# DeltaNet heads: the chunk output moved into the bank of values and state, the freed bank to the scores, three kinds of copies from VectorE to ScalarE

## The chip, the cores and the metric

One core of a Trainium2 chip. The metric is device microseconds (us) of one execution; 3 executions of the kernel before were timed. Engines: PE (TensorE, matmuls), DVE (VectorE), ACT (ScalarE), POOL (GpSimd), SP (SyncE, which issues most DMAs). Matmul results lie in PSUM, whose eight banks hold 512 fp32 numbers per partition each.

## What is computed

One step of a two-layer backbone: 128 context and 512 latent tokens, width 1024. Layer 0 runs softmax attention and a bidirectional gated DeltaNet side by side; layer 1 is a Mamba-2 mixer; each layer ends in an MLP. The change lies in the DeltaNet heads (four of them, key and value width 128). Per head and direction, over chunks:

```python
kb = k * beta[..., None]
m = where(strict, einsum('bnhid,bnhjd->bnhij', kb, k) * decay, 0.0)
t_mat = triangular_solve(eye + m, eye, lower=True, unit_diagonal=True)
u = t_mat @ (v * beta[..., None])
w = t_mat @ (kb * exp(gc)[..., None])
def step(s, inp):
    u_c, w_c, qk_c, qd_c, kd_c, dec_c = inp
    v_new = u_c - w_c @ s                  # the corrected values
    o_c = qd_c @ s + qk_c @ v_new          # the chunk's output
    s = s * dec_c[..., None, None] + einsum('bhcd,bhce->bhde', kd_c, v_new)
    return s, o_c
```

The kernel uses chunks of 128 tokens: one for the context, four for the latents. Then o is RMS-normalised and gated, laid beside the attention's output, and both go through one output projection.

## The kernel before

The large products (L287) are made of three passes, high and low parts of both operands, and PE is busy with them for most of the span. The change touches one stage, from about 225 to 525 us: four DeltaNet heads (`delta_head`, L768) are issued between the steps of the attention (`attention`, L1072, a generator) in the order 0, attention, 1, 2, 3 (the string in `even`). Heads 0 and 2 use one set of buffers and PSUM banks, heads 1 and 3 the other. A pool's buffer is given to the next tile when its last reader is done, so head 2 starts step by step as head 0 gives its tiles free.

Attention: per head pair a front (transposes L1114, scores L1124, maxima on DVE L1131 and L1136) and a back (scores again, L1154, exponentials on ACT, values L1182, and small products that close it, L1190 and L1198). Scores, their transposes and L1198 use the pool psc, which has two banks.

A head: matrix M (L806), inverse X by blocks (L821 to L924), w (L933), then eight steps, four chunks in both directions (L940 to L964): a bank `pv` takes v_new (L945, L946, both PE); DVE reads it twice, as vk (L949) and as vn (L951); L953 puts the state's product into the same bank and L955 adds it to the state; a bank of its own, `ops` of the one-bank pool pdno, takes the output (L957, L958), which ACT (L962) or DVE (L964) reads. The context's chunk follows (L969 to L982), then the finish: five squares (ACT L987), the reciprocal root (L988 and small DVE operations), scaling (DVE L996), transposes (PE L997) and the gate (DVE L998).

The output projection L287 needs weights split by ACT (L263) and DVE (L266), and operands split by ACT (L510) and DVE, among them the heads' outputs; head 2's end frees the room of operand 5. The reload of x (L663) is issued on ACT's queue.

The order of the instructions on each engine is set when the program is built, by a scheduler that simulates its own timeline (`schedule_with_timeline_sim`, L1617); the engines then work through their lists in order. Banks are given in the order of the pools. The stage before has pg1 (3 banks), pm1 (2, for the transposes `kvps`, L721), pmod1 (1) and pat0 (1).

Of the kernel before, what the change touches and what calls it, by code (L numbers as in the profile page):

```python
# [11 lines left out]
F32 = mybir.dt.float32  # L12
F32R = mybir.dt.float32r
I32 = mybir.dt.int32
AF = mybir.ActivationFunctionType
ALU = mybir.AluOpType
# [4 lines left out]
P = 128  # L21
# [171 lines left out]
class Prog:  # L193
# [393 lines left out]
    def even(self):  # L587
        nc, io = self.nc, self.io
# [6 lines left out]
        with ExitStack() as e1:  # L595
# [3 lines left out]
            with ExitStack() as e2:  # L599
# [14 lines left out]
                xs, half = self.modulate(0, ("gmix", 0), 0, 1, hp, xp, True, cuts=4, rbs=rbs)  # L614
# [4 lines left out]
                for b, (n, c0) in enumerate(blocks):  # L619
                    hi, lo = watt[0] if b == 0 else self.wpart(self.wload(("att", b), n, wa), 0, n, wa)  # L620
                    for t in range(NT):
                        ps = self.pg.tile([P, 512], F32, name="atps", tag="g")
                        for k in range(KT):
                            for q, (x, w) in enumerate(((xs[0], hi), (xs[0], lo), (xs[1], hi))):
                                nc.tensor.matmul(ps[:, :n], x[k][:, TOFF[t]:TOFF[t] + P], w[:, k, :],  # L625
                                                 start=k == 0 and q == 0, stop=k == KT - 1 and q == 2)
# [14 lines left out]
                    self.delta_in(tp, pm, h, xs, dn[h])  # L641
        self.share = False
        with eak, ExitStack() as e1:
            cp, *sets, self.pout, psc, pat, at = self.pools(
                e1, ("con2", 1, "right"), ("pdn0", 2, None), ("pdn1", 2, None), ("pdno", 1, None), ("psc", 2, None), ("pat", 1, None), ("at", 1, "left"))
            self.con2 = cp.tile([P, io["cst"].shape[1] - self.csmall], F32, name="con2")
            nc.scalar.dma_start(out=self.con2, in_=io["cst"][:, self.csmall:])
            sets = list(zip(self.pools(e1, ("dn1", 1, "right"), ("dn0", 1, "right")), sets))
            att = self.attention(at, psc, pat, qkv, keys, ota)
            for ch in "0abcdefghi123":  # L650
                if ch in "0123":
                    self.delta_head(*sets[1 - int(ch) % 2], int(ch), dn[int(ch)], gt)
                else:
                    for _ in range(AS):
                        next(att, None)
            for _ in att:
                assert False

        hes, xes, e1 = ExitStack(), ExitStack(), ExitStack()
# [12 lines left out]
        xs, half = self.modulate(0, ("gmlp", 0), 3, 4, hp, np_, False)  # L672
# [95 lines left out]
    def delta_head(self, dn, pd, h, st_, gt):  # L768
        nc, v, g = self.nc, self.nc.vector, self.nc.gpsimd
        qT, kk, vv, zs, rq = (st_[n] for n in ("q", "k", "v", "z", "rq"))  # L770
# [8 lines left out]
        X, Xt = (both(n) for n in ("X", "Xt"))  # L779
# [49 lines left out]
        qd = [dn.tile([P, 4, P], F32, name=f"qd{d}", tag=f"qd{d}") for d in range(2)]  # L829
# [8 lines left out]
        qk = [qk0, dt]  # L838
# [9 lines left out]
        def values(d, t):  # L848

            o = dn.tile([P, P], F32, name="vb", tag=f"vb{d}")  # L850
            nc.scalar.activation(out=o, in_=vv[:, t, :], func=AF.Copy, scale=gt["beta"][:, d, t, h:h + 1])
            return o
# [27 lines left out]
        for l in range(1, 5):  # L880
            py = bank()
            for t in range(NT):
# [3 lines left out]
                            in1=lev[:, l - 1:l, 0].rearrange("p o (b c) -> p o b c", c=32).to_broadcast(wide), op=ALU.mult)  # L886
# [3 lines left out]
            for e in range(2):  # L890
                v.scalar_tensor_tensor(out=Xtc[:, e], in0=pu[:, :NT * 64].rearrange("p (t e c) -> p t e c", e=2, c=32)[:, :, e, :],
                                       scalar=lvn[:, l - 1, e:e + 1], in1=Xtc[:, e], op0=ALU.mult, op1=ALU.add)
# [19 lines left out]
        half = lambda ps: ps[:, :NT * H].rearrange("p (t c) -> p t c", c=H)  # L912
        for d in range(2):
            a, b = hv[d], hv[1 - d]
# [4 lines left out]
        for d in range(2):  # L919
            a, b = hv[d], hv[1 - d]  # L920
            pz = bank()
            for t in range(NT):
                nc.tensor.matmul(pz[a, t * H:(t + 1) * H], W[a, t, a], Yc[a, t, b], start=True, stop=True)
            v.tensor_scalar(out=X[a, 1 - d, :, b], in0=half(pz)[a], scalar1=-1.0, scalar2=None, op0=ALU.mult)  # L924

        o = M
        wn = (Xt[:, 0], kT)
# [7 lines left out]
        st = []  # L935
# [4 lines left out]
        for n in range(4):  # L940
            for d in range(2):
                c = n if d == 0 else 3 - n
                t = c + 1
                pv = bank()
                nc.tensor.matmul(pv[:, 0:P], X[:, 1 - d, t, :], values(d, t), start=True, stop=False)  # L945
                nc.tensor.matmul(pv[:, 0:P], wn[d][:, t, :], st[d], start=False, stop=True)  # L946
                if n < 3:
                    vk = dn.tile([P, P], F32, name="vk", tag=f"vk{d}")
                    v.tensor_scalar(out=vk, in0=pv[:, 0:P], scalar1=gt["ek"][:, d, t, h:h + 1], scalar2=None, op0=ALU.mult)  # L949
                vn = dn.tile([P, P], F32, name="vn", tag=f"vn{d}", bufs=2)  # L950
                v.tensor_copy(vn, pv[:, 0:P])  # L951
                if n < 3:
                    nc.tensor.matmul(pv[:, P:2 * P], kk[:, t, :], vk, start=True, stop=True)  # L953
                    s = dn.tile([P, P], F32, name="s", tag=f"s{d}", bufs=2)
                    v.scalar_tensor_tensor(out=s, in0=st[d], scalar=dec[d][:, c:c + 1], in1=pv[:, P:2 * P], op0=ALU.mult, op1=ALU.add)  # L955
                po = self.pout.tile([P, 512], F32, name="ops", tag="o")
                nc.tensor.matmul(po[:, 0:P], qd[d][:, c, :], st[d], start=True, stop=False)  # L957
                nc.tensor.matmul(po[:, 0:P], qk[d][:, t, :], vn, start=False, stop=True)  # L958
                if n < 3:
                    st[d] = s  # L960
                if n < 2:
                    nc.scalar.activation(out=o[:, t, :], in_=po[:, 0:P], func=AF.Copy, scale=rq[:, t:t + 1])  # L962
                else:
                    v.scalar_tensor_tensor(out=o[:, t, :], in0=po[:, 0:P], scalar=rq[:, t:t + 1], in1=o[:, t, :], op0=ALU.mult, op1=ALU.add)  # L964

        vns = []
        for d in range(2):
            pv = bank()
            nc.tensor.matmul(pv[:, 0:P], X[:, 1 - d, 0, :], values(d, 0), start=True, stop=True)  # L969
            vk = dn.tile([P, P], F32, name="vk", tag=f"vk{d}")  # L970
            v.tensor_scalar(out=vk, in0=pv[:, 0:P], scalar1=gt["ek"][:, d, 0, h:h + 1], scalar2=None, op0=ALU.mult)
            vn = dn.tile([P, P], F32, name="vn0", tag=f"vn{d}", bufs=2)
            v.tensor_copy(vn, pv[:, 0:P])
            vns.append(vn)
            nc.tensor.matmul(pv[:, P:2 * P], kk[:, 0, :], vk, start=True, stop=True)
            s = dn.tile([P, P], F32, name="s0", tag=f"s{d}", bufs=2)
            nc.scalar.copy(out=s, in_=pv[:, P:2 * P])
            nc.sync.dma_start(out=self.io["o_sd"][d, h], in_=s)
        po = bank()
# [646 lines left out]
```

## Time and profile before

| | us |
|---|---|
| median of 3 executions | 2215.07 (2214.77 to 2222.48) |
| profiled execution, its own time | 2212.08 |
| its span | 2210.0 |
| PE busy | 2101.8 |
| DVE busy | 1340.5 |
| ACT busy | 911.9 |
| mean granted TensorE clock | 0.978 of full |

In the rows further down, "busy" is the time in which an engine had an instruction in work; PEld is the loading of weights, which goes on beside PE. PEclk is the clock granted to TensorE as a share of 2.4 GHz. "Idle before" is an engine's idle time just ahead of a group's instructions, with the operation that ended it. "x10" counts records; an fp32 matmul of this stage has two. Names such as dps (the heads' banks), scps (scores), kvps and ops are those of the tiles.

### The profile page before, as it was taken

What the parts mean: (1) busy time and instruction counts of PE and PEld (TensorE: products, weight loads), DVE (VectorE), ACT (ScalarE), POOL (GpSimd) and SP (SyncE); (2) the same over time, 40 slices, a digit from 0 to 9 for tenths busy, and PEclk for the clock granted to TensorE, in tenths of its full rate; (3) what the DMA queues carried; (4) which work ended last, traced back from release to release, by engine and by line L of the source; (5) the groups of instructions that cost most, each with busy time, mean ns of one, the idle gap of its engine ahead of it and who ended that gap; (6) DMA issues with size and microseconds to landing.
All of it is one profiled execution on the core that took longest, in us unless ns stands there. A gap on an engine that the chain in (4) does not pass through costs nothing.

```text
span 2210.0 us, 36682 instructions
## 1 busy us (share of the span) xinstructions
PE 2101.8 (95%) x15045; PEld 1982.5 (90%) x15045; DVE 1340.5 (61%) x2751; ACT 911.9 (41%) x1914; POOL 224.1 (10%) x138
## 2 busy tenths in 40 slices
PE   6999798999999999999989899999899999999997
PEld 5999686888899999999888788989899899999996
DVE  6486767655786777663767665676653733334344
ACT  4345445352532323242466566666521522222230
POOL 1041403100000000000111112222310000000000
PEclk9999898899999999999999999999999999999999
DMA  7351101003254444421245343444322221122211
GB/s 319 119 194 39 38 1 34 1 19 149 88 190 142 153 138 149 150 98 44 93 126 136 102 123 104 110 134 120 100 102 77 77 77 72 67 73 76 77 58 48
DMA packets 70792, 221.93 MB, mean 100 GB/s; under 512 B 6266, under 2 KB 39010, under 8 KB 49762
## 3 DMA queue, kind: packets, MB, share of 16 engines
q1 hardware_dynamic: 60464, 205.10, 28.0%
q10 hardware_dynamic: 10162, 14.50, 1.9%
q8 instruction: 118, 1.93, 0.4%
q14 instruction: 48, 0.39, 0.1%
HBM read 211.40 MB, written 8.18 MB: 99 GB/s over the span
## 4 chain that ended last, share of the span: by engine, by line
PE 79%; DVE 8%; DMA 7%; ACT 3%; issue 1%; SPq 1%; ACTq 0%; DVEq 0%; POOL 0%; POOLq 0%
PE gps L287 61%; DMA bc<-afs 3%; DMA Q<-afs 3%; PE atps L625 2%; PE avps L1182 2%; PE stps L448 1%; PE yps L1523 1%; DMA wraw<-wall 1%; ACT bc L1508 1%; PE scps L1124 1%; PE dps L883 1%; DMA X<-growd 1%; PE stps L1552 1%; PE dps L889 1%; PE modps L331 1%
## 5 line engine op out<-in xcount | busy, mean ns | idle before, releaser
L287 PE MATMUL gps<-hh,whi 128*128 128x322 f32 (+3 forms) x1552 | 493.3, 318 | 1.2 <-ACT whi L263 0.9
L287 PE MATMUL gps<-hh,wlo 128*128 128x322 f32 (+3 forms) x1552 | 489.4, 316 | 1.3 <-POOL wlo L266 0.8
L287 PE MATMUL gps<-hl,whi 128*128 128x322 f32 (+3 forms) x1552 | 487.4, 314 | 2.2 <-DVE hl L505 2.2
L263 ACT CAST whi<-wraw 128x1024 fp32r<-128x1024 f32 (+2 forms) x220 | 231.7, 1056 | 516.3 <-PE gps L287 493.3
L287 PE MATMUL gps<-hidh,whi 128*128 128x320 f32 x1024 | 317.4, 310 | 0.0
L287 PE MATMUL gps<-hidl,whi 128*128 128x320 f32 x1024 | 316.1, 309 | 0.0
L287 PE MATMUL gps<-hidh,wlo 128*128 128x320 f32 x1024 | 315.8, 308 | 0.0
L287 PE MATMUL gps<-yh,whi 128*128 128x320 f32 x1280 | 304.3, 309 | 1.8 <-ACT yh L1264 1.8
L287 PEld LDWEIGHTS gps<-hh,whi 128*128 128x128 f32 (+1 forms) x1552 | 294.1, 190 | 9.6 <-issue 6.0
L287 PEld LDWEIGHTS gps<-hl,whi 128*128 128x128 f32 (+1 forms) x1552 | 294.0, 189 | 6.4 <-DVE hl L505 3.2
L287 PEld LDWEIGHTS gps<-hh,wlo 128*128 128x128 f32 (+1 forms) x1552 | 294.3, 190 | 4.7 <-issue 2.5
L266 DVE TENSOR_TENSOR wlo<-wraw,whi 128x1024 fp32r<-128x1024 f32 (+1 forms) x185 | 230.8, 1249 | 73.2 <-ACT whi L263 72.8
L287 PE MATMUL gps<-yh,wlo 128*128 128x320 f32 x768 | 237.6, 310 | 0.0
L517 DVE SCALAR_TENSOR_TENSOR xt<-gps,mod,xt 128x128 f32<-128x128 f32 (+1 forms) x216 | 87.9, 436 | 227.4 <-PE gps L287 227.3
L287 PEld LDWEIGHTS gps<-yh,whi 128*128 128x128 f32 x1280 | 220.0, 188 | 3.6 <-ACT yh L1264 1.9
L287 PEld LDWEIGHTS gps<-hidh,whi 128*128 128x128 f32 x1024 | 192.1, 188 | 2.8 <-issue 1.6
L287 PEld LDWEIGHTS gps<-hidl,whi 128*128 128x128 f32 x1024 | 192.1, 188 | 1.0 <-issue 1.0
L287 PEld LDWEIGHTS gps<-hidh,wlo 128*128 128x128 f32 x1024 | 192.1, 188 | 0.0
L266 POOL TENSOR_TENSOR wlo<-wraw,whi 128x1024 fp32r<-128x1024 f32 (+1 forms) x35 | 93.2, 2663 | 950.1 <-ACT whi L263 933.4
L287 PEld LDWEIGHTS gps<-yh,wlo 128*128 128x128 f32 x768 | 144.9, 189 | 0.1
L352 DVE SCALAR_TENSOR_TENSOR macc<-wraw,condst,macc 128x512 f32<-128x512 f32 x196 | 136.9, 744 | 1.2 <-ACT macc L355 1.2
L530 DVE TENSOR_SCALAR hr<-gps 128x320 f32<-128x320 f32 x128 | 62.6, 489 | 109.4 <-PE gps L287 109.3
(398 smaller groups left out, 3338.7 us busy)
## 6 DMA issues: line engine op xcount, KB each, us to landing
wraw<-wall SPq DMA_DIRECT2D x158, 1024.0 KB, 4.9
bc<-afs SPq DMA_DIRECT2D x40, 512.0 KB, 6.5
Q<-afs SPq DMA_DIRECT2D x64, 128.0 KB, 7.2
xt<-xt ACTq DMA_DIRECT2D x2, 2560.0 KB, 11.6
X<-growd SPq DMA_DIRECT2D x8, 320.0 KB, 6.1
xd<-xt ACTq DMA_DIRECT2D x1, 2560.0 KB, 8.5
xt<-xd SPq DMA_DIRECT2D x1, 2560.0 KB, 10.3
S<-ss ACTq DMA_DIRECT2D x16, 128.0 KB, 2.2
```

The costliest lines, as they stand in the source:

```text
L263: self.nc.scalar.copy(out=hi, in_=raw[:, :, c:c + m])
L266: eng.tensor_tensor(out=lo, in0=raw[:, :, c:c + m], in1=hi.bitcast(F32), op=ALU.subtract)
L287: self.nc.tensor.matmul(ps, ws[k // KT][q // 2][:, k % KT, :], xs[q % 2][k][:, c], start=k == 0 and q == 0, stop=k == n - 1 and q == 2)
L331: nc.tensor.matmul(ps[32 * q:32 * q + 32], lhs, x[:, :, 32 * q:32 * q + 32], start=start, stop=stop)
L352: nc.vector.scalar_tensor_tensor(out=a, in0=x, scalar=w, in1=a, op0=ALU.mult, op1=ALU.add)
L448: pin = nc.tensor.matmul(ps[r:r + 32, :HU], self.ones32, sq, start=k < 4, stop=k >= nk - 4)
L517: self.nc.vector.scalar_tensor_tensor(out=x[:, dst], in0=ps[:, src], scalar=gate[:, m, q:q + 1], in1=x[:, dst], op0=ALU.mult, op1=ALU.add)
L530: nc.vector.tensor_scalar(out=r, in0=ps, scalar1=0.0, scalar2=None, op0=ALU.max)
L625: nc.tensor.matmul(ps[:, :n], x[k][:, TOFF[t]:TOFF[t] + P], w[:, k, :], start=k == 0 and q == 0, stop=k == KT - 1 and q == 2)
L883: nc.tensor.matmul(py[:, t * 32:(t + 1) * 32], m32[:, t, :], mixed(Xc, t, l), start=True, stop=True)
L889: nc.tensor.matmul(pu[:, t * 64:(t + 1) * 64], Yc[:, t, :], Xtc[:, :, t, :], start=True, stop=True)
L1182: nc.tensor.matmul(acc, val(c, i), p, start=c == 1, stop=c == 6)
```

## The change

The pool pdno goes; a chunk's output is written into columns 256 to 383 of the bank that holds v_new and the state's product. The freed bank is psc's third. The copy vn of the corrected values (L951, and L973 for the context) and the negated half of the inverse (L924) are made by ACT in place of DVE.

```diff
-            cp, *sets, self.pout, psc, pat, at = self.pools(
-                e1, ("con2", 1, "right"), ("pdn0", 2, None), ("pdn1", 2, None), ("pdno", 1, None), ("psc", 2, None), ("pat", 1, None), ("at", 1, "left"))
+            cp, *sets, psc, pat, at = self.pools(
+                e1, ("con2", 1, "right"), ("pdn0", 2, None), ("pdn1", 2, None), ("psc", 3, None), ("pat", 1, None), ("at", 1, "left"))
...
-            v.tensor_scalar(out=X[a, 1 - d, :, b], in0=half(pz)[a], scalar1=-1.0, scalar2=None, op0=ALU.mult)
+            nc.scalar.mul(out=X[a, 1 - d, :, b], in_=half(pz)[a], mul=-1.0)
...
-                v.tensor_copy(vn, pv[:, 0:P])
+                nc.scalar.copy(out=vn, in_=pv[:, 0:P])
...
-                po = self.pout.tile([P, 512], F32, name="ops", tag="o")
-                nc.tensor.matmul(po[:, 0:P], qd[d][:, c, :], st[d], start=True, stop=False)
-                nc.tensor.matmul(po[:, 0:P], qk[d][:, t, :], vn, start=False, stop=True)
+                po = pv[:, 2 * P:3 * P]
+                nc.tensor.matmul(po, qd[d][:, c, :], st[d], start=True, stop=False)
+                nc.tensor.matmul(po, qk[d][:, t, :], vn, start=False, stop=True)
...
-            v.tensor_copy(vn, pv[:, 0:P])
+            nc.scalar.copy(out=vn, in_=pv[:, 0:P])
```

Since the scheduler builds the order from the whole program, other instructions move too. Three places:

PE's list at the stage's start, where the last transposes `kvps` of the stage before (L721) meet the attention's first (L1114). Before:

```order
L721 MATMUL kvps<-con,dq_1012 128x128
L721 MATMUL kvps<-con,kt 128x128
L721 MATMUL kvps<-con,dq_1012 128x128
L721 MATMUL kvps<-con,kt 128x128
L1114 MATMUL scps<-con,pp 128x128
L721 MATMUL kvps<-con,vt 128x128 x2
L1114 MATMUL scps<-con,pp 128x128 x7
L788 MATMUL dps<-con,dk_1003 128x128 x5
L721 MATMUL kvps<-con,dq_1012 128x128
L721 MATMUL kvps<-con,kt 128x128
L721 MATMUL kvps<-con,vt 128x128
L1114 MATMUL scps<-con,pp 128x128 x2
```

The same place after:

```order
L721 MATMUL kvps<-con,dq_1012 128x128
L721 MATMUL kvps<-con,kt 128x128
L721 MATMUL kvps<-con,vt 128x128
L805 MATMUL dps<-kT 128x128 x5
L721 MATMUL kvps<-con,dq_1012 128x128
L721 MATMUL kvps<-con,kt 128x128
L721 MATMUL kvps<-con,vt 128x128
L721 MATMUL kvps<-con,dq_1012 128x128
L721 MATMUL kvps<-con,kt 128x128
L721 MATMUL kvps<-con,vt 128x128
L788 MATMUL dps<-con,dk_998 128x128 x5
L1114 MATMUL scps<-con,pp 128x128 x10
```

The attention's ten transposes stood between those of kvps; now all ten stand behind the last of them.

PE's list at the stage's end, from the heads' last products (L957, L958, L975, L981) and the attention's last ones (L1190, L1198) to the projection's first (L287). Before:

```order
L958 MATMUL ops<-vn,dt 128x128
L975 MATMUL dps<-vk,dk_1013 128x128
L1190 MATMUL scps<-con,au 128x1 x7
L981 MATMUL dps<-vn_5215,de 128x128
L957 MATMUL ops<-s,qd_4922 128x128
L958 MATMUL ops<-vn,de 128x128
L975 MATMUL dps<-vk,dk_1013 128x128
L981 MATMUL dps<-vn_5227,dt 128x128
L1198 MATMUL scps<-con,ar 64x128 x10
L957 MATMUL ops<-s,qd_4923 128x128
L958 MATMUL ops<-vn,dt 128x128
L287 MATMUL gps<-op,whi 128x320 x4
```

After, from the attention's last ones on; behind the rows shown the two heads' recurrences go on, and 88 products of L945, L946, L953, L957, L958, L969, L975 and L981 and ten transposes L997 stand in all between L933 and the first L287:

```order
L1198 MATMUL scps<-con,ar 64x128 x10
L933 MATMUL dps<-X,kT 128x128
L933 MATMUL dps<-X,Xt 128x128 x4
L945 MATMUL dps<-vb,X 128x128
L946 MATMUL dps<-s,Xt 128x128
L945 MATMUL dps<-vb,X 128x128
L946 MATMUL dps<-s,kT 128x128
L945 MATMUL dps<-vb,X 128x128
L946 MATMUL dps<-s,Xt 128x128
L945 MATMUL dps<-vb,X 128x128
L946 MATMUL dps<-s,kT 128x128
L953 MATMUL dps<-vk,dk_1013 128x128 x2
```

The last two heads' recurrences (the heads 2 and 3) stood between the attention's products; now they stand behind them and ahead of the projection.

ACT's list around the projection's first weights (L263), with the heads' squares (L987) and operand splits (L510). Before:

```order
L851 ACTIVATE vb<-dv_1014,beta 128x128
L977 COPY s_5218<-dps 128x128
L977 COPY s_5230<-dps 128x128
L982 ACTIVATE M<-dps,rq_1016 128x128
L987 ACTIVATE ojk,oss<-M 128x128
L510 CAST op<-ota_1020 128x640
L263 CAST whi<-wraw 128x1024 x2
L987 ACTIVATE ojk,oss<-M 128x128
L510 CAST op<-dq_1007 128x640
L263 CAST whi<-wraw 128x1024 x2
L987 ACTIVATE ojk,oss<-M 128x128 x3
L263 CAST whi<-wraw 128x1024
```

After:

```order
L977 COPY s_4791<-dps 128x128
L510 CAST op<-dq_997 128x640
L987 ACTIVATE ojk,oss<-M 128x128
L982 ACTIVATE M<-dps,rq_1011 128x128
L987 ACTIVATE ojk,oss<-M 128x128 x8
L510 CAST op<-dq_1012 128x640
L663 DMA xt<-xt 128x5120
L263 CAST whi<-wraw 128x1024 x4
L510 CAST op<-dq_1002 128x640
L510 CAST op<-dq_1007 128x640
L263 CAST whi<-wraw 128x1024
L446 ACTIVATE sq<-xt 128x320 x2
```

The first weights were split between one head's squares; now four weight splits stand behind both heads' squares, the split of a head's output (dq_1012) and the issue of x's reload (L663).

## Rows read from the trace of the kernel before

**Rows 1.** The page: the span, and the busiest engine's line.

```profile
span 2210.0 us, 36682 instructions
...
PE 2101.8 (95%) x15045; PEld 1982.5 (90%) x15045; DVE 1340.5 (61%) x2751; ACT 911.9 (41%) x1914; POOL 224.1 (10%) x138
```

**Rows 2.** Busy time by stage: stretch, its length, then busy us per engine, PEclk, DMA.

```profile
225.00:260.00 35.00, 24.10 (x127) 20.15 (x127) 29.20 (x66) 13.99 (x46) 16.48 (x14) 0.80 0.19 59
260.00:327.00 67.00, 64.73 (x494) 54.55 (x494) 46.58 (x122) 31.12 (x71) 7.07 (x5) 1.00 0.00 1
327.00:396.00 69.00, 61.22 (x352) 50.37 (x352) 49.75 (x140) 33.80 (x91) 19.53 (x15) 0.85 0.10 28
396.00:468.00 72.00, 71.63 (x517) 61.49 (x516) 46.28 (x124) 30.12 (x72) 5.12 (x4) 0.93 0.00 1
468.00:503.00 35.00, 35.00 (x223) 28.00 (x224) 19.15 (x70) 18.87 (x51) 0.00 (x0) 1.00 0.25 97
503.00:525.00 22.00, 18.11 (x120) 16.96 (x116) 15.00 (x35) 8.76 (x19) 0.00 (x0) 0.92 0.46 170
```

**Rows 3.** Busy time by stage, around the second pair of heads.

```profile
380.00:390.00 10.00, 7.99 (x30) 6.38 (x30) 8.07 (x28) 1.77 (x7) 3.14 (x2) 0.50 0.00 0
390.00:400.00 10.00, 10.00 (x62) 9.64 (x61) 6.64 (x13) 2.41 (x5) 4.63 (x3) 0.55 0.01 2
```

**Rows 4.** Chain of waits: start, length, what (x counts records).

```profile
275.45 1.06 PE dps L889 x10
...
341.34 5.17 DMA X<-growd
...
366.10 5.86 DMA X<-growd
```

**Rows 5.** Groups by line: busy, mean ns, idle before and its releasers.

```profile
L1124 PE MATMUL scps<-kst,qs 128*128 128x512 f32 (+2 forms) x72 | 37.1, 526 | 8.5 <-DVE mx L1131 4.7 <-DVE mx L1136 3.8
...
L1154 PE MATMUL scps<-qs,kst 128*128 128x512 f32 (+1 forms) x56 | 28.9, 519 | 3.8 <-DVE mx L1136 3.8
...
L851 ACT ACTIVATE vb<-dv,beta 128x128 f32<-128x128 f32 x38 | 14.8, 400 | 9.2 <-PE dps L945 8.3 <-PE dps L946 0.5
...
L951 DVE COPY vn<-dps 128x128 f32<-128x128 f32 x32 | 8.9, 281 | 2.2 <-PE dps L946 2.0
...
L962 ACT ACTIVATE M<-ops,rq 128x128 f32<-128x128 f32 x16 | 5.9, 366 | 8.9 <-PE ops L958 8.8
...
L924 DVE TENSOR_SCALAR X<-dps 64x320 f32<-64x320 f32 x8 | 3.9, 489 | 1.3 <-PE dps L923 1.2
...
L977 ACT COPY s<-dps 128x128 f32<-128x128 f32 x8 | 2.1, 260 | 6.7 <-PE dps L975 6.7
```

**Rows 6.** Timeline: how head 2 is finished, and the projection's first weights.

```profile
482.08 0.36 ACT L982 ACTIVATE M<-dps,rq 128x128 f32<-128x128 f32 x1
...
482.58 0.32 ACT L987 ACTIVATE ojk<-M 128x128 f32<-128x128 f32 x1
...
484.88 0.19 ACT L987 ACTIVATION_READ_ACCUMULATOR ojk<-M 128x1 f32 x1
...
485.10 0.17 DVE L988 TENSOR_SCALAR oss<-oss 128x5 f32<-128x5 f32 x1 [2.09 <-ACT ojk L987]
...
488.75 1.06 DVE L996 TENSOR_SCALAR M<-M,oro 128x128 f32<-128x128 f32 x5
...
493.67 0.34 ACTq L663 DMA_DIRECT2D xt<-xt  x1
...
494.46 0.73 ACT L510 CAST op<-dq 128x640 fp32r<-128x640 f32 x1
...
506.35 1.99 ACT L263 CAST whi<-wraw 128x1024 fp32r<-128x1024 f32 x2
```

**Rows 7.** Chain of waits at the stage's end.

```profile
502.63 1.05 PE scps L1198 x16
...
508.40 12.41 PE gps L287 x73
```

More of the change, by code (lines that the diff above doesn't have):

```diff
@@ L961, in delta_head @@
                 if n < 2:
-                    nc.scalar.activation(out=o[:, t, :], in_=po[:, 0:P], func=AF.Copy, scale=rq[:, t:t + 1])
+                    nc.scalar.activation(out=o[:, t, :], in_=po, func=AF.Copy, scale=rq[:, t:t + 1])
                 else:
-                    v.scalar_tensor_tensor(out=o[:, t, :], in0=po[:, 0:P], scalar=rq[:, t:t + 1], in1=o[:, t, :], op0=ALU.mult, op1=ALU.add)
+                    v.scalar_tensor_tensor(out=o[:, t, :], in0=po, scalar=rq[:, t:t + 1], in1=o[:, t, :], op0=ALU.mult, op1=ALU.add)
         vns = []
```

## The prediction

> **What bounds the kernel now.** I read the busy line of the page first: PE has 2101.8 of 2210.0 us [rows 1], so PE's work, which the change leaves as it is, sets the time, and the change can only add or take away idle time of PE or a lower clock. The view by stage is next, for where PE idles between 225 and 525 us [rows 2]. PE is full in three stretches (260 to 327, 396 to 468, 468 to 503: idle 2.3, 0.4 and 0.0). It idles 10.9 us in 225 to 260, where DVE is busy 29.20 of 35, and 7.8 us in 327 to 396, where the second pair of heads begins and DVE is busy 49.75 of 69; it idles 3.9 us in 503 to 525, where the projection begins. In 380 to 400 the clock is 0.50 and 0.55 of full while PE is busy 18.0 of 20 us [rows 3]: it is at the lower of its two levels (1.2 GHz) for most of that, which costs about half of the busy time, 9 us. The chain of waits shows two loads of X at 341 and 366 us, 5.17 and 5.86 us long [rows 4]; they can start only when an earlier head has read its X for the last time. Ahead of the score products PE waits 8.5 and 3.8 us for the maxima on DVE, 12.3 together; that is what a third score bank could touch [rows 5].
>
> **The change part by part.**
>
> Copies. DVE loses 40 copies of vn (32 by L951, the context's 8 taken at the same price) at 0.281 us, 11.2 us, and 8 negations L924 at 0.489, 3.9 us: 15.1 us [rows 5]. ACT gains them. The trace has no vn on ACT; its nearest row is ACT's copy out of PSUM of the same size, L977, 0.260 us [rows 5]; the upper bound is L510 with 640 columns, 0.73 [rows 6]. I take 0.26 for vn, since shape and source are the same, and for L924 with 320 columns 0.44, by a straight line between the two: 10.4 + 3.5 = 13.9 us. In the stage ACT is busy 137 of 300 us, so it is hidden there; with the cover gone it costs up to 13.9. What the relief of DVE brings counts only where DVE sets the pace. Of the 278 us in which the heads run, 327 to 396 has 69, so 15.1 x 69 / 278 = 3.7 us; bounds 0 and the whole idle time there, 7.8. I take -3.7.
>
> The output in the values' bank. The bank is held longer, by L957, L958 and the read L962: 0.42 + 0.37 us (a product of this stage takes 1.06 / 5 = 0.212, [rows 4]; L962 in [rows 5]). From L945 to L962 that makes 0.42 + 0.28 + 0.21 + 0.42 + 0.37 = 1.7 us for one direction of one step. The new wait stands on PE: L958 behind ACT's copy, and behind it in PE's list the next head's or the attention's products. A head has two banks, one for each direction, and one step of both directions gives PE 10 products, 2.1 us, so even a head by itself hides the hold; two heads side by side hide it twice. I take 0; if ACT is late by one L851 (0.400, [rows 5]) in each of the 32 steps it is +12.8; below nothing there is only the old bank's own wait, 8.8 us by L962's row, but that is idle time of ACT, not of PE.
>
> The third score bank. Bounds 0 and -12.3. DVE, which makes the maxima, is busy 83% of the first stretch, so a further bank lets PE run ahead by one tile but makes DVE no faster. I take a third, -4.1. Its first bank lies where the transposes kvps had their second, and in the new order the attention's transposes stand behind the last of these: eight that stood ahead, 8 x 0.212 = +1.7 (bounds 0 and 2.1). In DVE's new list the early parts of both first heads stand ahead of the last maxima: bounds 0 and what DVE has free in 225 to 260, 5.8; I take +2, since the attention's matmuls can fill part of it.
>
> The tail. This is the large one. Before, the attention's last products L1198 end at 503.7 and the projection starts at 508.4 [rows 7]; the recurrences of heads 2 and 3 lie under the attention, and head 2 is finished from 482 on [rows 6] while PE is full (468 to 503 has no idle time, [rows 2]). In the new order 5 products L933, 88 of the recurrences and the context chunk and ten transposes stand between the last L1198 and the first L287, without attention products between them. Of that PE has 98 x 0.212 = 20.8 us of work (five transposes run inside the finish below). The wait for the last results of a recurrence, with nothing beside it, is an estimate: vk, L953, state, L957 and L958, output (0.28 + 0.21 + 0.28 + 0.42 + 0.37 = 1.6), then the context's vb, L969, vk, L975, copy (0.40 + 0.21 + 0.28 + 0.21 + 0.26 = 1.4), 3.0 together. Then the finish: L982 0.36; eight squares still to come, at 0.5 each by the five from 482.58 to 485.07, 4.0; the reciprocal root from L988 at 485.10 to L996 at 488.75, 3.65, with the other head's small operations between them 4.0; L996 of both heads 2 x 1.06; L998, which has no row here, as the 640 columns of L510, 0.73; the split L510 0.73; the issue of x's reload 0.34; one weight block L263 1.0. That is 13.3 [rows 6]. The weights come last because in ACT's new list they stand behind the squares, the split and the reload's issue, which waits for head 2's transposes. So L287 starts 1.1 + 18.7 + 3.0 + 13.3 = 36 us behind the last L1198, and PE idles 36.1 - 20.8 = 15.3 of it. Before it idled 3.9 in 503 to 525. The tail costs +11.4. Nothing else can fill it, as the lists are worked in order.
>
> Perfetto Trace Analysis of the Trainium skill, Optimization Strategy, says that regimes with different limits may run better interleaved. The rows agree: the stretch in which recurrence and attention were mixed has PE at 35.00 of 35 [rows 2]; by that rule taking them apart costs, as the sum has it.
>
> Sum: 11.4 - 3.7 - 4.1 + 1.7 + 2.0 = +7.3. The profiled execution took 2212.1 (its span and 2.1 around it), so 2219.4; that execution lies 3.0 under the median shown, which makes 2222.4.
>
> **The rivals.**
>
> R1, faster. DVE's relief and the third bank clear the middle: the 12.3 of waits for maxima, the 7.8 of idle PE in 327 to 396 and with them the lower clock (9.0) go: -29.1 + 11.4 + 1.7 + 2.0 = -14.0, 2201.1. For it speaks that the same two waits recur for every score tile and that the clock falls just where PE has idled. Against it: the second pair waits for loads of X too [rows 4], which no bank hastens, and the maxima remain DVE's. It decides if more than 18 of the 29 us go. The same page of the Trainium skill, same section, says that a bubble that keeps coming back can mean too little PSUM. That is this mechanism; the trace here names DVE's maxima as the releaser, which fits a lack of banks as well as a slow DVE.
>
> R2, slower by more. In the tail each product waits for ACT or DVE, PE idles between them, and its clock falls to 1.2 GHz as at 380 [rows 3]: the 18.7 us double, +26.0, 2241.1. For it: at 380 to 390 PE was busy 8 of 10 us and had 0.50. Against it: with products of the same kind in 260 to 327 the clock stayed at 1.00 [rows 2], though attention filled it there. TensorE: Matmul & The Clock Gate of the Trainium skill, Part 1, calls the throttled state the default, and activity what releases it; the 0.50 behind idle PE agrees.
>
> R3, nothing moves. The third stretch gives back what the tail costs, because head 2 and 3 side by side share waits: 0, 2215.1. For it: idle PE of 7.8 and 10.9 stands ready to be filled. Against it: four terms would have to cancel.
>
> **How the numbers follow.** A difference under 0.5%, 11 us, is no change. The forecast has 0.44 (own range -4 to +18, 2211 to 2233: faster 0.01, same 0.26, slower 0.17); R1 0.25 (faster 0.20, same 0.05); R2 0.20 (slower 0.19, same 0.01); R3 0.11 (same 0.10, faster 0.01). Together faster 0.22, same 0.42, slower 0.36. The range 2200 to 2240 takes in the middle of R1 and all but the upper half of R2.
>
> **What the profile after would show.** Right: L951 on ACT at 0.26 to 0.27 us; the last L1198 near 479 (503.7 - 20.8 - 4.1) and the first L287 some 36 us later, with PE busy about 21 of these; the ten L1114 behind the last kvps; L1124's and L1154's waits for maxima at 8 us together; DVE's busy time 15 lower. R1 shows 380 to 400 at full clock and the last L1198 ahead of 470; R2 a PEclk near 0.5 in the tail. Wrong is the forecast if PE idles under 8 us between the last L1198 and L287, or if the attention ends no earlier than before.

## The result, and the profile after

The changed kernel takes 2241.70 us (median of 5; before 2215.84 in its five): 1.0116 of before, 95% interval 1.0098 to 1.0134. The forecast was 2222.4 (+7.3 us), with a difference within 0.5% the likeliest, and the range 2200 to 2240. The loss is +25.9 us: the direction was forecast, the size is three and a half times the forecast one, and the time lies outside the range. The page of after:

```profile
span 2239.9 us, 36683 instructions
...
PE 2119.7 (95%) x15045; PEld 1998.3 (89%) x15045; DVE 1335.2 (60%) x2703; ACT 924.0 (41%) x1962; POOL 221.3 (10%) x138
```

The span is 29.9 us longer. By the end of the output projection (its last product ends at 574.8 before, 598.4 after) 23.6 us are lost. How long the rest takes, which the change leaves alone, varies from one profiled execution to the next (1632 to 1649 us over all kernels below), so the traces are compared at that point. Busy time by stage of after, for [rows 2]:

```profile
225.00:260.00 35.00, 20.17 (x105) 16.00 (x103) 29.20 (x57) 15.49 (x47) 19.89 (x16) 0.78 0.20 58
260.00:327.00 67.00, 64.31 (x369) 55.62 (x370) 41.17 (x97) 23.32 (x54) 2.63 (x2) 0.81 0.00 1
327.00:396.00 69.00, 64.59 (x453) 54.23 (x452) 37.50 (x100) 39.66 (x115) 7.72 (x6) 0.95 0.10 28
396.00:468.00 72.00, 65.43 (x391) 54.14 (x392) 57.06 (x123) 25.54 (x59) 17.23 (x13) 0.88 0.00 1
468.00:503.00 35.00, 34.74 (x256) 25.76 (x256) 12.21 (x49) 20.82 (x51) 0.00 (x0) 1.00 0.17 61
503.00:525.00 22.00, 18.28 (x156) 17.59 (x154) 11.86 (x39) 15.39 (x63) 0.00 (x0) 0.98 0.05 13
```

To be seen: PE idles 4 us more in the first stretch; the second is as busy as before but its clock is 0.81 in place of 1.00; the fourth has 6.6 idle us in place of 0.4. The third, which held 7.8 idle us and the low clock, got better. So the loss begins at the start. The attention's first transposes on PE, before and then after:

```profile
226.29 0.27 PE L1114 MATMUL scps<-con,pp 128*128 128x128 f32 x1
```

```profile
235.08 1.28 PE L1114 MATMUL scps<-con,pp 128*128 128x128 f32 x10
```

They start 8.8 us later. The attention's first back opens with L1148, on PE before and then after:

```profile
260.14 1.28 PE L1148 MATMUL scps<-con,nm 128*128 128x128 f32 x10
```

```profile
274.02 2.48 PE L1148 MATMUL scps<-con,nm 128*128 128x128 f32 x10
```

It is 13.9 us late and runs at half speed. It needs the maxima, and these need DVE; the first maxima (L1131) start 10.6 us late. DVE before (the first maxima, and the scaling of a head's keys, L732), then after:

```profile
235.73 1.01 DVE L1131 TENSOR_REDUCE mx<-scps 128x2 f32<-128x256 f32 x2
...
254.39 1.06 DVE L732 TENSOR_SCALAR dk<-dk,drs 128x128 f32<-128x128 f32 x5
```

```profile
240.07 5.50 DVE L732 TENSOR_SCALAR dk<-dk,drs 128x128 f32<-128x128 f32 x5
245.50 0.88 DVE L806 TENSOR_TENSOR M<-dps,M 128x512 f32<-128x512 f32 x2
246.29 1.01 DVE L1131 TENSOR_REDUCE mx<-scps 128x2 f32<-128x256 f32 x2
```

The five L732 stood behind the maxima and took 1.06 us; now they stand ahead of them and take 5.50. POOL is what differs beside them, before and after:

```profile
249.78 1.34 POOL L793 TENSOR_TENSOR Xt<-X,gc 128x640 f32<-128x640 f32 x1
258.80 2.79 POOL L835 TENSOR_TENSOR qd<-qd,dq 128x512 f32<-128x512 f32 x2 [7.68 <-DVE dec L834]
```

```profile
240.11 1.54 POOL L800 TENSOR_TENSOR M<-M,de 128x640 f32<-128x640 f32 x1 [3.69 <-ACT de L796]
241.60 1.27 POOL L798 TENSOR_TENSOR M<-db,con 128x640 f32<-128x640 f32 x1
242.95 1.32 POOL L799 TENSOR_TENSOR M<-M,beta 128x640 f32<-128x640 f32 x1
244.23 1.26 POOL L793 TENSOR_TENSOR Xt<-X,gc 128x640 f32<-128x640 f32 x1
```

Before, POOL idled from 251.1 to 258.8; after, it worked all through. The Trainium skill, SBUF — State Buffer, Who interferes with whom, says that a `tensor_scalar`, which L732 is, can run in a mode that needs a port pair shared with GpSimd, and that then the one that issues first holds the pair for its whole instruction while the other waits. The trace agrees: about 1.1 us for each L732 (5.50 / 5), near POOL's 1.3 for one of its own, against 0.21 (1.06 / 5) with POOL idle.

Meanwhile PE's clock fell. In pieces of 5 us (PE's busy time is the second figure behind the stretch, PEclk the third from the end), before:

```profile
240.00:245.00 5.00, 3.12 (x18) 2.32 (x18) 4.92 (x14) 2.03 (x6) 0.53 (x1) 1.00 0.24 66
...
255.00:260.00 5.00, 5.00 (x25) 4.61 (x25) 4.60 (x12) 2.59 (x7) 1.20 (x2) 0.60 0.00 0
...
280.00:285.00 5.00, 5.00 (x39) 4.57 (x37) 3.15 (x5) 0.60 (x1) 0.00 (x0) 1.00 0.00 0
```

And after:

```profile
240.00:245.00 5.00, 2.31 (x8) 1.57 (x7) 5.00 (x6) 1.28 (x2) 4.81 (x4) 0.50 0.00 2
...
280.00:285.00 5.00, 5.00 (x27) 5.00 (x26) 1.19 (x3) 1.45 (x3) 0.00 (x0) 0.50 0.00 0
...
290.00:295.00 5.00, 5.00 (x31) 3.87 (x31) 2.85 (x6) 1.23 (x3) 0.00 (x0) 1.00 0.00 0
```

Before, the clock is at its lower level mainly between 250 and 260 and full from there to 327; after, it is 0.50 in five of the ten pieces between 240 and 290, and below 0.9 in all ten.

The tail, on PE after: the attention's last product, the heads' last, the transposes, the projection's first; and the same by stretch, for [rows 7]:

```profile
497.06 1.31 PE L1198 MATMUL scps<-con,ar 128*64 128x128 f32 x20
...
520.89 0.39 PE L981 MATMUL dps<-vn,dt 128*128 128x128 f32 x2
526.85 1.37 PE L997 MATMUL dps<-con,M 128*128 128x128 f32 x5 [5.57 <-DVE M L996]
529.35 1.30 PE L997 MATMUL dps<-con,M 128*128 128x128 f32 x5 [1.13 <-DVE M L996]
532.21 1.85 PE L287 MATMUL gps<-op,whi 128*128 128x320 f32 x4 [1.56 <-ACT whi L263]
```

```profile
498.40:521.40 23.00, 22.62 (x186) 21.42 (x186) 14.37 (x41) 15.70 (x55) 0.00 (x0) 1.00 0.02 7
521.40:532.20 10.80, 2.67 (x10) 1.79 (x10) 8.48 (x43) 5.13 (x23) 0.00 (x0) 0.64 0.16 37
532.20:537.00 4.80, 4.74 (x16) 4.34 (x17) 4.80 (x5) 4.06 (x5) 0.00 (x0) 0.50 0.84 350
```

### The profile page after: what moved, and what is told of

The parts are those of the page before. It is cut to its first block, busy times and chain, and to the rows that moved or that the text cites. A ratio compares the mean times of both kernels' runs of the same rounds, so it can differ in the third digit from the quotient of the medians.

```text
span 2239.9 us, 36683 instructions
## 1 busy us (share of the span) xinstructions
PE 2119.7 (95%) x15045; PEld 1998.3 (89%) x15045; DVE 1335.2 (60%) x2703; ACT 924.0 (41%) x1962; POOL 221.3 (10%) x138
## 4 chain that ended last, share of the span: by engine, by line
PE 79%; DVE 8%; DMA 7%; ACT 4%; issue 1%; SPq 1%; ACTq 0%; DVEq 0%
PE gps L287 61%; DMA bc<-afs 3%; PE atps L625 2%; DMA Q<-afs 2%; PE avps L1182 2%; PE yps L1523 1%; PE stps L448 1%; ACT bc L1508 1%; DMA wraw<-wall 1%; PE scps L1124 1%; PE dps L883 1%; PE modps L331 1%; DMA X<-growd 1%; PE dps L889 1%; PE stps L1552 1%
## 5 line engine op out<-in xcount | busy, mean ns | idle before, releaser
L287 PE MATMUL gps<-hh,whi 128*128 128x322 f32 (+3 forms) x1552 | 495.7, 320 | 0.5 <-ACT whi L263 0.5
L287 PE MATMUL gps<-hh,wlo 128*128 128x322 f32 (+3 forms) x1552 | 492.6, 318 | 1.3 <-POOL wlo L266 0.8
L287 PE MATMUL gps<-hl,whi 128*128 128x322 f32 (+3 forms) x1552 | 490.0, 316 | 2.2 <-DVE hl L505 2.2
L263 ACT CAST whi<-wraw 128x1024 fp32r<-128x1024 f32 (+2 forms) x220 | 232.1, 1059 | 524.3 <-PE gps L287 496.1
L287 PE MATMUL gps<-hidh,whi 128*128 128x320 f32 x1024 | 317.4, 310 | 0.0
L287 PE MATMUL gps<-hidl,whi 128*128 128x320 f32 x1024 | 316.1, 309 | 0.0
L287 PE MATMUL gps<-hidh,wlo 128*128 128x320 f32 x1024 | 315.8, 308 | 0.0
L287 PE MATMUL gps<-yh,whi 128*128 128x320 f32 x1280 | 304.6, 309 | 1.8 <-ACT yh L1264 1.8
L287 PEld LDWEIGHTS gps<-hh,whi 128*128 128x128 f32 (+1 forms) x1552 | 296.8, 191 | 8.8 <-issue 5.7
L287 PEld LDWEIGHTS gps<-hl,whi 128*128 128x128 f32 (+1 forms) x1552 | 296.2, 191 | 6.4 <-DVE hl L505 3.2
L287 PEld LDWEIGHTS gps<-hh,wlo 128*128 128x128 f32 (+1 forms) x1552 | 296.7, 191 | 4.7 <-issue 2.5
L287 PE MATMUL gps<-yh,wlo 128*128 128x320 f32 x768 | 237.5, 310 | 0.0
L517 DVE SCALAR_TENSOR_TENSOR xt<-gps,mod,xt 128x128 f32<-128x128 f32 (+1 forms) x216 | 88.2, 437 | 234.7 <-PE gps L287 234.5
L287 PEld LDWEIGHTS gps<-yh,whi 128*128 128x128 f32 x1280 | 219.9, 188 | 3.6 <-ACT yh L1264 1.9
L287 PEld LDWEIGHTS gps<-hidh,whi 128*128 128x128 f32 x1024 | 192.1, 188 | 2.8 <-issue 1.6
L287 PEld LDWEIGHTS gps<-hidl,whi 128*128 128x128 f32 x1024 | 192.1, 188 | 1.0 <-issue 1.0
L287 PEld LDWEIGHTS gps<-hidh,wlo 128*128 128x128 f32 x1024 | 192.1, 188 | 0.0
L287 PEld LDWEIGHTS gps<-yh,wlo 128*128 128x128 f32 x768 | 144.9, 189 | 0.1
```

The source lines that it names most:

```text
L263: self.nc.scalar.copy(out=hi, in_=raw[:, :, c:c + m])
L287: self.nc.tensor.matmul(ps, ws[k // KT][q // 2][:, k % KT, :], xs[q % 2][k][:, c], start=k == 0 and q == 0, stop=k == n - 1 and q == 2)
L517: self.nc.vector.scalar_tensor_tensor(out=x[:, dst], in0=ps[:, src], scalar=gate[:, m, q:q + 1], in1=x[:, dst], op0=ALU.mult, op1=ALU.add)
```

## The experiments

Each row: time as a ratio to before's runs on the same chip (medians 2218 to 2221 us; 2215.8 for the row after), its 95% interval, and from the trace the starts of the first L1148 and of the projection, and the projection's end, in us. A trace is one execution, and need not be the median one. Times in us that an expectation gives were meant for a before of 2215 to 2220 us.

| run | ratio | interval | L1148 | proj. starts | ends |
|---|---|---|---|---|---|
| before | 1 | | 260.1 | 507.4 | 574.8 |
| after | 1.0116 | 1.0098-1.0134 | 274.0 | 532.2 | 598.4 |
| copies | 1.0008 | 0.9992-1.0024 | 261.9 | 511.3 | 578.2 |
| bank3 | 1.0082 | 1.0063-1.0101 | 273.4 | 527.0 | 593.1 |
| b_late | 1.0110 | 1.0084-1.0136 | 271.8 | 529.0 | 595.5 |
| after2 | 1.0092 | 1.0065-1.0120 | 276.2 | 533.6 | 601.0 |
| afterpat | 1.0038 | 1.0020-1.0055 | 252.0 | 518.5 | 583.6 |
| after732 | 1.0046 | 1.0028-1.0064 | 264.7 | 517.5 | 583.1 |
| pat2 | 1.0058 | 1.0038-1.0077 | 260.9 | 523.2 | 588.4 |
| p2gate1 | 1.0032 | 1.0015-1.0050 | 261.8 | 508.6 | 578.6 |
| apgate1 | 1.0039 | 1.0024-1.0053 | 251.9 | 515.7 | 582.5 |
| b_swap | 1.0046 | 1.0025-1.0068 | 261.6 | 512.3 | 578.7 |
| pat2vn1 | 1.0104 | 1.0086-1.0121 | 259.7 | 519.1 | 598.7 |
| apvn1 | 1.0131 | 1.0105-1.0156 | 249.1 | 520.1 | 600.9 |
| after732g | 1.0068 | 1.0045-1.0092 | 264.8 | 514.4 | 584.2 |
| b732 | 1.0013 | 0.9997-1.0030 | 261.4 | 509.6 | 576.6 |
| p2g732 | 1.0026 | 1.0011-1.0041 | 261.1 | 515.8 | 583.3 |
| apg732 | 1.0024 | 1.0009-1.0040 | 252.3 | 515.5 | 582.0 |

**The parts.** copies is before with the diff's last three kinds of lines; bank3 is after without them.

> Only the three kinds of copies go to ScalarE; banks and pools stay as before. Theory A (the loss is in the new order of the lists, brought by the banks: a late start of the attention, some 15 us, and the last two heads' recurrences alone behind the attention, some 12 us): the order of PE stays nearly as before, 2211 to 2219 us. Theory B (the copies on ScalarE delay L957 and L953, which wait for vn): 2223 us or more, with idle PE ahead of L958 put down to vn on ACT. Theory C (relief of VectorE pays): under 2209 us.

> Only the banks of the change: the output in the values' bank and three score banks, of which the first was the transposes' second; the three kinds of copies stay on VectorE. Theory A1 (the score bank's place, and the finish ahead of the projection, make the loss): 1.009 to 1.014 of before, as the whole change, first L1148 at 270 to 276 us. Rival (the copies on ScalarE and the banks cost together what neither does alone): under 1.007.

The copies alone cost nothing that can be measured, and relieving DVE brought nothing. The banks alone cost 0.8%. That is a little under the 0.9% expected and below the whole change's 1.16% (the intervals overlap by a little), so a small part may need both.

**Where the score bank lies.** b_late changes nothing in before but two pools' order; afterpat does the reverse in after.

```diff
b_late:   ("pdno", 1, None), ("psc", 2, None)  ->  ("psc", 2, None), ("pdno", 1, None)
afterpat: ("psc", 3, None), ("pat", 1, None)   ->  ("pat", 1, None), ("psc", 3, None)
```

> The kernel before with only the order of two pools exchanged, so that the scores' first bank is the second bank of the transposes kvps, as in the changed kernel; nothing else is changed. In PE's list all score transposes L1114 then stand behind the last kvps. Theory A1 (this bank alone delays the attention's start): first L1148 near 274 us in place of 260, idle time and lower clock 13 to 18 us more by 300 us, 1.005 to 1.009 of before (2231 to 2240 us where before has 2220). Rival (the start is late because the heads run side by side from the beginning, freed from the shared output bank): first L1148 near 260, 0.998 to 1.003.

> The change with the pools pat and psc exchanged: the same number of banks each, but the scores' first bank is no longer the transposes' second one. In PE's list ten score transposes L1114 stand ahead of the last kvps again; behind the last L1198 stand 179 products. Theory A: the start's part of the loss goes (first L1148 near 260 to 264 us) and the tail's stays: 2226 to 2233 us. Theory B: 2238 to 2244 us.

The start moved as theory A said in both, late in b_late and early in afterpat; there L1148 came still earlier than the 260 to 264 expected, but at half clock. b_late lost more than theory A1 gave. L1148 in b_late and in afterpat:

```profile
271.81 2.48 PE L1148 MATMUL scps<-con,nm 128*128 128x128 f32 x10
```

```profile
252.02 2.47 PE L1148 MATMUL scps<-con,nm 128*128 128x128 f32 x10 [8.24 <-DVE nm L1140]
```

Exchanging two pools costs before 1.1% by itself, with its old copies, its separate output bank and its two score banks (the output bank moves with them). Its tail is as short as before's (the last L1198 ends at 524.8, L287 starts at 529.0), so its 20.7 us are lost ahead of the tail. Putting the score banks elsewhere takes about two thirds of the loss from after.

**The stretched operation.** after732 moves only L732 to ACT.

```diff
-v.tensor_scalar(out=dn["k"][:, t, :], in0=dn["k"][:, t, :], scalar1=rs[:, 1, t:t + 1], ...)
+nc.scalar.activation(out=dn["k"][:, t, :], in_=dn["k"][:, t, :], func=AF.Copy, scale=rs[:, 1, t:t + 1])
```

> The changed kernel with one more operation on ScalarE: the scaling of the keys L732, five instructions per head, which in the changed kernel took VectorE 5.50 us in place of 1.06 while GpSimd worked, ahead of the first maxima. Theory A4 (the first maxima are late because these stretched operations stand ahead of them on VectorE): the first L1131 some 4 to 6 us earlier, first L1148 at 266 to 271 us in place of 274, 1.006 to 1.010 of before. Rival (the maxima are late because the scores are): first L1148 at 273 or later, 1.010 or more.

More than expected. DVE and PE of after732:

```profile
241.08 0.89 DVE L806 TENSOR_TENSOR M<-dps,M 128x512 f32<-128x512 f32 x2 [1.51 <-POOL M L800]
241.88 1.22 DVE L1131 TENSOR_REDUCE mx<-scps 128x2 f32<-128x256 f32 x2
```

```profile
264.69 1.35 PE L1148 MATMUL scps<-con,nm 128*128 128x128 f32 x10 [0.50 <-DVE nm L1140]
```

The first maxima come 4.4 us earlier, L1148 9.3, at full clock, and the projection ends 15.3 us earlier, though the scores' transposes stand where after has them (they start at 234.5). What the late scores leave is 6.1 us at the first maxima and 4.6 at L1148, against before; the larger part of the 13.9 went with DVE work that had slipped ahead of the maxima and stretched there. The other late runs have it too: the five L732 took 5.50 us in bank3 and 4.18 in b_late and in after2, ahead of the first L1131, and 1.06 or 1.07 in every other run that has them on DVE. POOL worked beside them in those four traces with a late start and idled in the other nine. In b_late:

```profile
241.93 4.18 DVE L732 TENSOR_SCALAR dk<-dk,drs 128x128 f32<-128x128 f32 x5
```

The list of after732 differs elsewhere too, so the 15.3 us are not shown to be all that one wait's.

The same line in before:

> The kernel before with the scaling of the keys L732 on ScalarE and nothing else. Theory A4 (the operation matters where it stands stretched ahead of the first maxima, which it does not here: it takes 1.06 us and stands behind them): 0.998 to 1.002 of before. Rival (VectorE's relief by itself pays in this stage, wherever the maxima stand): 0.993 to 0.997.

As theory A4 expected: before, where the operation isn't stretched, gains nothing that can be measured.

**The third score bank and the tail.** Two kernels have two score banks.

```diff
after2: ("psc", 3, None), ("pat", 1, None)  ->  ("psc", 2, None), ("pat", 1, None)
pat2:   ("psc", 3, None), ("pat", 1, None)  ->  ("pat", 2, None), ("psc", 2, None)
```

> The change with two score banks in place of three; the freed bank is given to nobody (the score banks then are banks 4 and 5, the first of which was the second one of the transposes kvps). In PE's list the first scores still stand behind the last kvps, but only 10 products, the transposes L997, stand between the last L1198 and the first L287. Theory A: the tail's part of the loss goes, the start's part stays: about 2228 us (2222 to 2234), first back product L1148 still near 274 us. Theory B (ACT's copies and the longer hold of the banks): as after, 2238 to 2244 us.

> The change with the freed bank given to the attention's value products (pat 2, psc 2, pat first). PE's list has the score transposes ahead of the last kvps and 13 products in the tail. Theory A: both parts go, 2212 to 2221 us; the longer hold of the banks costs under 5 us. Theory B: 2230 us or more. Theory C: under 2209 us.

Theory A missed both. The times (2240.5 and 2230.7 us) lie in theory B's ranges, but copies, at 1.0008, doesn't bear out ACT's copies as the cause. after2 has the attention, not the recurrences, at the end, and the intervals leave open whether it is faster than after at all. The start stayed late, as said, and its clock stayed low longer: 0.50 from 275 to 305, where after's rose near 289. pat2 starts as early as before but loses 13.6 us by the projection's end: I had counted products in the tail, and not the finish. On PE in pat2:

```profile
508.62 1.31 PE L1198 MATMUL scps<-con,ar 128*64 128x128 f32 x20
...
515.46 1.35 PE L997 MATMUL dps<-con,M 128*128 128x128 f32 x5 [4.67 <-DVE M L996]
...
520.37 1.30 PE L997 MATMUL dps<-con,M 128*128 128x128 f32 x5 [3.56 <-DVE M L996]
...
523.22 1.85 PE L287 MATMUL gps<-op,whi 128*128 128x320 f32 x4 [1.56 <-ACT whi L263]
```

The heads 2 and 3 end together and nothing covers either finish. p2gate1 keeps head 3 behind head 2's second step; apgate1 does so in afterpat, after732g in after732.

```diff
-nc.tensor.matmul(pv[:, 0:P], X[:, 1 - d, t, :], values(d, t), start=True, stop=False)
+with self.tc.issue_after(self.hold) if h == 3 and n == 0 else nullcontext(): nc.tensor.matmul(pv[:, 0:P], X[:, 1 - d, t, :], values(d, t), start=True, stop=False)
...
-nc.tensor.matmul(po, qk[d][:, t, :], vn, start=False, stop=True)
+last = nc.tensor.matmul(po, qk[d][:, t, :], vn, start=False, stop=True).ins; self.hold = last if n <= 1 else self.hold
```

> The kernel of the run pat2 (1.0058 of before) in which head 3's first product L945 may stand in PE's list only behind head 2's second recurrence step; no buffer is shared. In PE's list L945 of head 3 ends ahead of the projection, its transposes L997 stand inside it. Theory A2 (heads 2 and 3 ending together expose the whole finish, some 8 us, ahead of L287): idle time ahead of L287 falls from 9.8 to 3 to 6 us in 500 to 525, 1.001 to 1.004 of before. Rival (the finish is exposed whatever the heads' order): 1.005 to 1.008.

> The same hold on head 3 in the kernel of the run afterpat (1.0038 of before, three score banks with the first one elsewhere). Theory A2: 0.999 to 1.002 of before. Rival: 1.003 or more.

> The changed kernel with the scaling of the keys L732 on ScalarE (run after732: 1.0046 of before) and with the hold on head 3 of the run p2gate1. Theory A (late start and exposed finish are the two causes, and little else): 1.000 to 1.003 of before; idle time and lower clock in 500 to 550 under 6 us, where after732 had 13.0. Rival (the hold only moves idle time into the projection or before it): 1.004 or more.

In p2gate1, as theory A2 said, the projection starts at 508.6, head 3's transposes stand inside it, at 523, and PE idles 3.2 us in 500 to 525 in place of 9.8. The projection ends 9.8 us earlier than in pat2; the times, 1.0032 and 1.0058, have overlapping intervals. With three score banks the same hold gained nothing: the projection started 3 us earlier, and ended 1 us earlier in apgate1 and 1 us later in after732g. There the rival was right.

Before with the heads' two memories exchanged:

```diff
-sets = list(zip(self.pools(e1, ("dn1", 1, "right"), ("dn0", 1, "right")), sets))
+sets = list(zip(self.pools(e1, ("dn1", 1, "right"), ("dn0", 1, "right"))[::-1], sets))
```

> The kernel before with the SBUF memory of heads 0 and 2 exchanged with that of heads 1 and 3; PSUM and all operations as before. Theory A2 (the projection's first weights and the reload of x lie in head 2's memory, so the projection starts when head 2 is finished; if its place is that of the head that ends last, the whole finish of a head stands between the attention and the projection): idle PE of 9 to 14 us ahead of the first L287, behind L997 of head 3; 1.003 to 1.007 of before. Rival (the projection waits for its operands and weights' transfers, whatever the memory): 0.998 to 1.002.

This makes the projection of before wait for all heads' transposes (the last L997 at 509.4, L287 at 512.3), and costs 0.46%; the wait is 7.0 us of idle PE in 500 to 525 in place of 3.9, less than expected, and the projection ends only 3.9 us later. Its runs spread widely (2213.6 to 2239.7 us), and the one traced is the fastest of them, so the cost is known poorly.

pat2 and afterpat with a buffer that all heads share (pvn is the pool of con2):

```diff
-vn = dn.tile([P, P], F32, name="vn", tag=f"vn{d}", bufs=2)
+vn = self.pvn.tile([P, P], F32, name="vn", tag="vnx", bufs=1)
```

> The kernel of the run pat2 (1.0058 of before) in which the four heads share one SBUF buffer for the corrected values vn of the latent chunks, where each had its own four. Theory A3 (the one output bank was what kept the heads apart; another buffer that all heads share does it as well): heads finish one after the other again, the last head's recurrence stands inside the projection, the idle time of 14 us ahead of L287 goes: 0.998 to 1.003 of before. Rival (the longer hold of the heads' banks costs what pat2 lost): 1.005 or more.

> The kernel of the run afterpat (1.0038 of before; three score banks) with the same shared buffer for vn. Theory A3: the finish ahead of L287 is covered by the last head's recurrence inside the projection: 0.994 to 1.001 of before. Rival: 1.003 or more. A third score bank that pays shows as a value under that of the run pat2vn1.

The shared buffer was a bad way to keep heads apart: the last recurrence ran so late (its last L945 at 533 us) that its finish left PE idle inside the projection (in pat2vn1 PE is busy 3.4 of the 10 us from 535 to 545). Both times lie in the rivals' ranges. The theory that the old output bank kept the heads apart is neither shown nor refuted by it.

p2gate1 and apgate1 with the line of after732:

> The run p2gate1 (1.0032 of before) with the scaling of the keys on ScalarE: the freed bank is with the attention's value products, the start is early, head 3 is held. Theory A: 0.998 to 1.004 of before, within the interval of p2gate1. Rival (VectorE's relief pays): under 0.998.

> The run apgate1 (1.0039 of before; three score banks, early start, head 3 held) with the scaling of the keys on ScalarE. Theory A: 1.000 to 1.004. Rival (the third score bank pays once VectorE is free ahead of the maxima): under 0.998.

Both lie in theory A's ranges. With two score banks and with three the times agree (1.0026 and 1.0024), so no gain of the third one is to be seen. Neither beats before; none of the sixteen does.

## Why the prediction was wrong, by its steps

- **The copies.** Prices put at 0.26 and 0.44 us; measured:

```profile
L951 ACT COPY vn<-dps 128x128 f32<-128x128 f32 x32 | 8.1, 262 | 1.5 <-DVE vk L949 1.1
L924 ACT ACTIVATE X<-dps 64x320 f32<-64x320 f32 x8 | 3.5, 432 | 2.9 <-PE dps L923 2.7
```

  Right. What they were to bring, -3.7 us, is not there: the run copies has 1.0008. DVE's busy time fell by 5.3 (1340.5 to 1335.2), not 15: the one stretched group L732 took 4.4 of it back.
- **The longer hold of the bank**, 0: p2gate1, which has it, ends the projection 0.4 us behind copies. Its time, 1.0032 against 1.0008, leaves some 5 us unexplained, so 0 is likely but not shown.
- **The third score bank**, 8 us of waits for maxima left, has this row for [rows 5]:

```profile
L1124 PE MATMUL scps<-kst,qs 128*128 128x512 f32 (+2 forms) x72 | 36.4, 519 | 8.0 <-DVE mx L1136 4.3 <-ACT qs L1115 2.3 <-DVE mx L1131 1.3
L1154 PE MATMUL scps<-qs,kst 128*128 128x512 f32 (+1 forms) x56 | 28.2, 504 | 2.5 <-DVE mx L1136 2.5
```

  4.3 + 1.3 + 2.5 = 8.1. The row was right and of no use: no run with the third bank beats before.
- **The start, +1.7 + 2.0: the step that failed.** I had seen both things in the order, the transposes behind kvps and head work ahead of the maxima. I priced the first by the products' own time (8 x 0.212), where its cost is the wait behind the last kvps: the attention's transposes started 8.8 us later. I priced the second by DVE's free time, with rows whose durations held for POOL idle, where the five L732 took 5.50 us in place of 1.06. Together they made L1148 13.9 us late, and PE's lower clock followed, for which the sum had no term. afterpat and after732, each mending the start another way, end the projection 14.8 and 15.3 us earlier.
- **The tail**: L287 put 36 us behind L1198; measured 33.8 (498.4 to 532.2). (Before, the projection's first product starts at 507.4; the 508.4 of [rows 7] is where the chain goes over to it.) Right in kind, too large in idle time: 8.5 us (0.4 + 8.1), not 15.3. PE's work was put too low: 25.3 us (22.62 + 2.67), not 20.8, as the 0.212 a product came from L889 with 64 columns, and the 93 products here took 22.62 / 93 = 0.243. The 3.0 us of last waits were filled by the other head, and the finish took 10.8, not 13.3. With the first products at half clock (4.8 us) the tail cost, by estimate, some 4.6 + 2.4 = 7 us and not 11.4.
- **The attention's end**, 479: it was 498.4. The sum fell here. Up to the last L1198 PE was busy 257.4 of 278.7 us at 0.92 before and 244.9 of 273.4 at 0.88 after: idle time and lower clock together 42 and 58 us by this estimate, so the terms ahead of the tail, put at -4.1, came to about +16. The prediction's own signs of being wrong (under 8 us idle in the tail, an attention that ends no earlier) did not come, at 8.5 us and 5.3 us earlier: they watched the tail, and the loss was at the start.
- **R2** gave 2241.1 and the time is 2241.7, but that is luck, as its mechanism is refuted: the products of the tail ran at 1.00. The lower clock came between 240 and 289. R1 was half right that 380 to 400 would leave the low clock (0.89 and 0.67, from 0.50 and 0.55) and wrong that this decides.

Open: after the start is mended some 8 us remain with three score banks (afterpat, apgate1, after732), which no run took away. That a loss is the exposed finish is seen in pat2's trace alone. Why the clock stayed low as long as it did is open too.

## To carry to other kernels

When a program orders the lists, a freed PSUM bank is also a moved one: look up which work last used the bank that the first tile of the next stage will get, and read the new list there before pricing the gain. A duration of a VectorE row holds only for what GpSimd did beside it; a row that moves next to GpSimd work is priced, as the upper bound, with one duration of GpSimd's added to its own (the slowest L732 here took 1.66 us beside operations of up to 1.54). Count an exposed finish by what releases the next stage, not by the products left in a list.

## What was not expected of the hardware

PE can be busy without a gap and stay at 1.2 GHz for long. In b_late:

```profile
265.00:270.00 5.00, 2.21 (x14) 1.63 (x12) 4.94 (x14) 0.21 (x1) 1.82 (x2) 0.80 0.00 0
270.00:275.00 5.00, 5.00 (x25) 5.00 (x25) 1.22 (x3) 0.93 (x2) 0.00 (x0) 0.50 0.00 0
...
295.00:300.00 5.00, 5.00 (x13) 2.93 (x13) 2.16 (x5) 2.13 (x6) 0.00 (x0) 0.50 0.00 0
300.00:305.00 5.00, 5.00 (x31) 4.48 (x29) 2.26 (x6) 0.83 (x2) 0.00 (x0) 0.79 0.00 0
```

After a stretch with PE busy 2.21 of 5 us the clock was 0.50 and stayed there for 30 us in which PE had no idle time; it rose between 300 and 305, behind the attention's value products. after2 does the same from 275 to 305. So after a gap of a few us about half of those 30 us was lost (an estimate from the two levels). What brought the clock back is not shown.
